# State-space stage of a two-block model: paired head products, a third weight buffer, exponents formed by ScalarE, convolutions in another PSUM pair, the gate applied ahead of the norm

## The chip, the cores and the metric

The kernel runs on one core of one Trainium2 chip. The metric is device time in microseconds (us) of one execution, as the median of several runs. The engines are TensorE (PE for its matmuls, PEld for its weight loads), VectorE (DVE), ScalarE (ACT), GpSimd (POOL) and the queue engine SyncE (SP), which issues every transfer here.

## The reference

The input is a sequence of 512 tokens of width 1024. A first block of two layers (windowed attention, two recurrent mixers, a gated feed-forward part) is followed by a second block of two layers. Each layer of the second block has three branches that are gated and added; the first is a state-space branch, and nearly all of the change lies there:

```python
def _ssd_branch(z, xbc, dt_raw, conv_w, conv_b, dt_bias, a_log, d_skip, norm_w):
    xbc = jax.nn.silu(_centred_dwconv(xbc, conv_w, conv_b))      # 5 taps
    xs, bm, cm = ...                                             # 32 heads of 64; 4 groups of state 128
    dt = softplus(dt_raw + dt_bias)                              # 2 directions x 32 heads
    y_fwd = _ssd_scan(xs * dt[fwd], dt[fwd] * a[0], bm, cm)      # chunks of 128 tokens
    y_bwd = flip(_ssd_scan(flip(...)))
    y = y_fwd + y_bwd + d_skip * xs
    return _rmsnorm(y * silu(z), norm_w)
# in _ssd_scan, within a chunk: y_diag = (C B^T * exp(cum_q - cum_s)) x, causal
# across chunks:                y_off  = exp(cum) * C state
# in second_block: merged = sigmoid(gate) * (y_ssd @ w_br_ssd) + two other branches
```

## The kernel before

Activations are kept with features on the partitions and the 512 tokens along the free dimension. A projection (`proj`, `gemm_fm`) makes one tile of 128 features: its weights are loaded as one `wraw` tile of 128x1024 by SP, `split` makes a high part `whi` (a cast on ACT, L396) and a low part `wlo` (a subtraction on DVE, L397), and PE runs 24 matmuls (three for each of 8 pieces of the contraction, L403 to L405) into a PSUM bank. There are three `wraw` buffers and two buffers each for `whi` and `wlo`. PSUM has three rings: `pg` of 2 banks (all projections), `pm` of 4 banks and `pb` of 2 banks.

The state-space stage (`ssd`) of a layer has these parts:

- `decays`: a small projection for the step sizes, the running sums of the decays, and their copies in DRAM (`d_fe`, `d_eo`) and token-major in SBUF (`tm`: `fet`, `dtt`, `dst`).
- `conv_x(g)` and `conv_bc(g)`: projections of 4 and 2 feature tiles for group g, each followed by `conv`: one ACT instruction out of PSUM (L1343), four DVE taps that read the same PSUM bank (L1348), and a Silu (L1349). All use the `pg` ring.
- `prelude(g)`: transposes (`pb` ring), the products C B^T masked both ways (`cbl`, `cbu`), and the recurrence over chunks (`xd`, L1473; the matmul L1475; `shd` and `shs`).
- `ftiles(g)`: four feature tiles of two heads each. A feature tile makes a `z` projection, and for each of its two heads (j = 0, 1) it loads two rows of running sums broadcast to 128 partitions (`rf`, `re`, 256 KB each, L1502 and L1503), forms the exponent tile `t1` chunk by chunk (POOL: row minus column for one direction, L1507; DVE: the other direction and the minimum of both, L1508), forms `t2` as the masked products with the step sizes (POOL L1509, DVE L1510), takes the exponential (ACT, L1511), multiplies (DVE, L1512), and runs four matmuls of 128x64 weights and 128 columns into the half `64 * j` of the partitions of one PSUM bank (L1515). After both heads come the skip term (L1518), the part across chunks (matmuls L1524, DVE L1527, POOL L1528), the gate with silu(z) (POOL L1531), the split of the result into `syp` (ACT L1533, DVE L1534) and its square (ACT L1540).
- `branch(g)`: the projection of the group's four tiles to the 8 tiles of `merged` (weights `ws`, DVE L1554 adds out of PSUM).
- At the end the norm's factor is made into a broadcast tile `rb`. L1576 (POOL) multiplies the eight gate tiles by it, and L1577 (DVE) multiplies `merged` by the result.

`weave` sets the order in which instructions are written: `ftiles(g)` together with `conv_x(g + 1)`, or for the last group with the eight gate projections; then `conv_bc(g + 1)`; then `prelude(g + 1)` together with `branch(g)`. A planner with a cost model then orders each engine's instructions, so that what is ready may run ahead of what was written earlier; on the chip each engine keeps that order. Attention in the first block has one line that the change touches, the product with the values at L1166.

Of the kernel before, what the change touches and what calls it, by code (L numbers as in the profile page):

```python
# [214 lines left out]
def bc(ap, axis, n):  # L215
# [21 lines left out]
    "scd": 1, "stm": 3, "svy": 2, "sbm": 1, "scm": 2, "sxf": 7, "sbt": 1, "scl": 1, "scu": 1, "sxt": 4, "sxd": 2, "shs": 6, "shd": 2,  # L237
    "seo": 1, "srf": 2, "sre": 2, "sy1": 1, "so1": 1, "szs": 3, "syp": 5, "sqa": 1, "ssq": 1,
# [42 lines left out]
class Core:  # L281
    def __init__(self, tc, es, wflat, wat):
        self.tc, self.nc = tc, tc.nc
        self.wflat, self.wat = wflat, wat
        self.sb = es.enter_context(tc.tile_pool(name="sb", bufs=1))
        self.cur, self.opened = None, []
        self.use("N")
        self.dr = es.enter_context(tc.tile_pool(name="dr", bufs=1, space=bass.MemoryType.DRAM))
        self.n = 0
        self.rr = 0  # L290

# [83 lines left out]
    def load(self, key, kt, stay=False, eng=None, bufs=4):  # L375

        raw = self.raw(key, "wraw", 3)
        shape = [P, self.wat[key][1]]
        if stay:
            hi, lo = (self.w(shape, F32R, name=t, b=bufs) for t in ("wkh", "wkl"))  # L380
        else:
            hi, lo = (self.keep(t, [P, W_SLOT], F32R, bufs=2)[:, : shape[1]] for t in ("whi", "wlo"))
        self.split(raw, hi, lo, eng)
        v = lambda a: a.rearrange("p (k c) -> p k c", k=kt)
        return v(hi), v(lo)
# [79 lines left out]
def block1(c: Core, io, consts, finish, kvs, stop=None):  # L465
# [619 lines left out]
    def mixer_a(l, raw, av, mixed, shared):  # L1085
# [64 lines left out]
        def values(t, w):  # L1150
            kts = [t - 1, t] if t else [t]
            for kv in range(2):
# [11 lines left out]
                for j in range(2):  # L1164
                    for i, u in enumerate(kts):
# [155 lines left out]
def block2(c: Core, io, C, h, out, kvs, stop=None):  # L1321
# [29 lines left out]
    def proj(l, key, h):  # L1351
        ps = c.pg()
        c.gemm_fm(c.load(key, KD), h, ps)
        return ps
# [10 lines left out]
    def decays(l, h, cdr, tm, d_fe, d_eo):  # L1365
# [45 lines left out]
        for k, src in enumerate((fe, dtT, ds_)):  # L1411
# [3 lines left out]
            V.tensor_copy(tm[k], pt)  # L1415
            yield

    def ssd(l, h, merged):
# [10 lines left out]
        def conv_x(g):  # L1429
            for i in range(4):  # L1430
                o = c.w(name="sxf")
                conv(proj(l, ("xbc", l, 4 * g + i), h), cw, cb, 4 * g + i, o)
# [9 lines left out]
        def prelude(g):  # L1442
# [25 lines left out]
            for n in range(3):  # L1468
                for d in range(2):
                    ch = (n, 3 - n)[d]  # L1470
                    r0 = 32 * d + 8 * g
                    xd = c.w(name="sxd")
# [14 lines left out]
        def ftiles(g):  # L1487
            s = grp[g]
            xf, xt, hs, cmf, cbl, cbu = s["xf"], s["xt"], s["hs"], s["scm"], s["cbl"], s["cbu"]
            for i in range(4):  # L1490
                f = 4 * g + i
                eo = c.w([P, 2, S], name="seo")
                for d in range(2):
                    for j in range(2):
                        nc.sync.dma_start(eo[64 * j : 64 * j + 64, d], d_eo[32 * d + 2 * f + j].partition_broadcast(64))
                zs = c.w(name="szs")
                A.activation(zs, proj(l, ("z", l, f), h), AF.Silu)
                py = c.pm()
                for j in range(2):
# [4 lines left out]
                    t1, t2 = c.w(name="st1"), c.w(name="st2")  # L1504
                    for ch in range(NT):
                        sl = slice(ch * P, (ch + 1) * P)
                        G.tensor_scalar(t1[:, sl], re[:, sl], -1.0, fet[:, ch, 32 + hh : 33 + hh], op0=ALU.mult, op1=ALU.add)  # L1507
                        V.scalar_tensor_tensor(t1[:, sl], rf[:, sl], fet[:, ch, hh : hh + 1], t1[:, sl], op0=ALU.subtract, op1=ALU.min)  # L1508
                        G.tensor_scalar(t2[:, sl], cbl[:, ch], dtt[:, ch, hh : hh + 1], 1.0, op0=ALU.mult, op1=ALU.mult)  # L1509
                        V.scalar_tensor_tensor(t2[:, sl], cbu[:, ch], dtt[:, ch, 32 + hh : 33 + hh], t2[:, sl], op0=ALU.mult, op1=ALU.add)  # L1510
                    A.activation(t1, t1, AF.Exp)  # L1511
                    V.tensor_tensor(t2, t1, t2, op=ALU.mult)  # L1512
                    for ch in range(NT):
                        sl = slice(ch * P, (ch + 1) * P)
                        T.matmul(py[64 * j : 64 * j + 64, sl], xt[ch][:, i * P + 64 * j : i * P + 64 * j + 64], t2[:, sl], start=True, stop=True)  # L1515
                    yield
                y1 = c.w(name="sy1")
                V.scalar_tensor_tensor(y1, xf[i], C(f"dsk{l}")[:, f : f + 1], py, op0=ALU.mult, op1=ALU.add)  # L1518
                for d in range(2):
# [7 lines left out]
                    V.tensor_tensor(o1, po.rearrange("p n t -> p (n t)"), eo[:, d, sl], op=ALU.mult)  # L1527
# [31 lines left out]
        with c.phase("ssd"):  # L1559
# [13 lines left out]
            rb = c.w(name="srb", b=1)  # L1573
            V.tensor_copy(rb, rbp)
            for m in range(KD):
                G.tensor_tensor(gates[m], gates[m], rb, op=ALU.mult)  # L1576
                V.tensor_tensor(merged[m], merged[m], gates[m], op=ALU.mult)  # L1577

# [528 lines left out]
```

## Time and profile before

| | |
|---|---|
| Time, median of 3 runs (lowest to highest) | 3928.01 us (3925.15 to 3929.15) |
| The profiled execution | 3929.44 us; its span from first to last instruction 3927.6 us |
| Busy over the span | PE 3667.1 us (93%), DVE 2471.0 us (63%), ACT 1655.0 us (42%), POOL 891.4 us (23%) |
| Mean granted clock of TensorE | 0.974 of full speed |
| State-space stage | about 1590 to 2085 us in the first layer of the second block, 2775 to 3285 us in the second |

A fp32 matmul of this kernel stands as two instructions in the trace, one of the `whi`/`wlo` projections as one. Busy time is the union of instructions, and matmuls overlap at their ends, so a busy PE is not one at its peak.

### The profile page before, as it was taken

What the parts mean: (1) busy time and instruction counts of PE and PEld (TensorE: products, weight loads), DVE (VectorE), ACT (ScalarE), POOL (GpSimd) and SP (SyncE); (2) the same over time, 40 slices, a digit from 0 to 9 for tenths busy, and PEclk for the clock granted to TensorE, in tenths of its full rate; (3) what the DMA queues carried; (4) which work ended last, traced back from release to release, by engine and by line L of the source; (5) the groups of instructions that cost most, each with busy time, mean ns of one, the idle gap of its engine ahead of it and who ended that gap; (6) DMA issues with size and microseconds to landing.
All of it is one profiled execution on the core that took longest, in us unless ns stands there. A gap on an engine that the chain in (4) does not pass through costs nothing. (4 is left out here: it accounts for less than half of the span.)

```text
span 3927.6 us, 51381 instructions
## 1 busy us (share of the span) xinstructions
PE 3667.1 (93%) x19000; PEld 3002.9 (76%) x19000; DVE 2471.0 (63%) x4543; ACT 1655.0 (42%) x2650; POOL 891.4 (23%) x1133
## 2 busy tenths in 40 slices
PE   6889999998889999899999999998989999999997
PEld 5776887787768888677777787877777777787877
DVE  7976645567665333778766674337677866765337
ACT  5432422245324223544444564333444444655333
POOL 1331000003210000245542111004245542111003
PEclk9989999999799999999999999999999999999999
DMA  6611445642113223443433332322443433332222
GB/s 192 188 54 46 142 158 191 207 141 68 33 49 110 97 97 102 121 135 118 135 108 99 97 105 81 102 81 97 149 128 129 129 113 98 104 100 81 102 81 86
DMA packets 167564, 437.64 MB, mean 111 GB/s; under 512 B 30096, under 2 KB 41744, under 8 KB 167312
## 3 DMA queue, kind: packets, MB, share of 16 engines
q1 hardware_dynamic: 167312, 434.34, 35.0%
q8 instruction: 150, 2.46, 0.3%
q14 instruction: 102, 0.84, 0.1%
HBM read 400.96 MB, written 12.32 MB: 105 GB/s over the span
## 5 line engine op out<-in xcount | busy, mean ns | idle before, releaser
L403 PE MATMUL pg<-h,whi 128*128 128x512 f32 x2624 | 1057.0, 403 | 58.1 <-ACT whi L396 27.1
L405 PE MATMUL pg<-h,wlo 128*128 128x512 f32 x2624 | 1039.9, 396 | 13.9 <-DVE wlo L397 13.8
L404 PE MATMUL pg<-h,whi 128*128 128x512 f32 x2624 | 1037.5, 395 | 3.4 <-POOL h L397 3.4
L396 ACT CAST whi<-wraw 128x1024 fp32r<-128x1024 f32 (+1 forms) x532 | 552.1, 1039 | 1144.7 <-PE pg L404 927.0
L397 DVE TENSOR_TENSOR wlo<-wraw,whi 128x1024 fp32r<-128x1024 f32 (+1 forms) x532 | 701.1, 1319 | 435.9 <-ACT whi L396 423.9
L403 PEld LDWEIGHTS pg<-h,whi 128*128 128x128 f32 x2624 | 497.8, 190 | 176.1 <-ACT whi L396 41.3
L405 PEld LDWEIGHTS pg<-h,wlo 128*128 128x128 f32 x2624 | 497.5, 190 | 131.1 <-DVE wlo L397 25.8
L404 PEld LDWEIGHTS pg<-h,whi 128*128 128x128 f32 x2624 | 498.3, 190 | 112.0 <-POOL h L397 6.5
L397 POOL TENSOR_TENSOR gp<-mraw,gp 128x256 fp32r<-128x256 f32 x32 | 26.1, 833 | 866.5 <-ACT gp L396 866.5
L403 PE MATMUL pg<-whi,h 128*128 128x256 f32 (+1 forms) x640 | 189.6, 298 | 11.2 <-ACT whi L396 8.6
L404 PE MATMUL pg<-wlo,h 128*128 128x256 f32 (+1 forms) x640 | 187.6, 294 | 9.9 <-DVE wlo L397 9.8
L405 PE MATMUL pg<-whi,h 128*128 128x256 f32 (+1 forms) x640 | 185.4, 290 | 0.0
L1509 POOL TENSOR_SCALAR st<-scl,stm 128x128 f32<-128x128 f32 x256 | 121.9, 491 | 203.8 <-DVE scl L1463 127.7
L1507 POOL TENSOR_SCALAR st<-sre,stm 128x128 f32<-128x128 f32 x256 | 117.1, 469 | 199.3 <-DMA sre<-dram 124.6
L405 PE MATMUL pg<-gp,wlo 128*128 128x512 f32 (+1 forms) x432 | 160.0, 370 | 0.9 <-DVE wlo L397 0.9
L403 PE MATMUL pg<-gp,whi 128*128 128x512 f32 (+1 forms) x432 | 159.7, 370 | 0.0
L404 PE MATMUL pg<-gp,whi 128*128 128x512 f32 (+1 forms) x432 | 159.6, 369 | 0.0
L1348 DVE SCALAR_TENSOR_TENSOR svy<-pg,c,svy 128x510 f32<-128x510 f32 x192 | 142.5, 742 | 18.3 <-ACT svy L1343 16.9
L403 PE MATMUL pg<-yp,whi 128*128 128x512 f32 (+1 forms) x384 | 144.8, 379 | 4.8 <-ACT yp L396 2.9
L405 PE MATMUL pg<-yp,wlo 128*128 128x512 f32 (+1 forms) x384 | 144.4, 378 | 4.0 <-DVE wlo L397 4.0
L404 PE MATMUL pg<-yp,whi 128*128 128x512 f32 (+1 forms) x384 | 144.5, 377 | 3.7 <-DVE yp L397 3.7
L403 PEld LDWEIGHTS pg<-whi,h 128*128 128x128 f32 x640 | 125.9, 198 | 18.2 <-ACT whi L396 10.8
(558 smaller groups left out, 6733.5 us busy)
## 6 DMA issues: line engine op xcount, KB each, us to landing
wraw<-in_wflat_dram SPq DMA_DIRECT2D x596, 512.0 KB
srf<-dram SPq DMA_DIRECT2D x64, 256.0 KB
sre<-dram SPq DMA_DIRECT2D x64, 256.0 KB
seo<-dram SPq DMA_DIRECT2D x128, 128.0 KB
araw<-in_wflat_dram SPq DMA_DIRECT2D x16, 512.0 KB
rsw<-rr SPq DMA_DIRECT2D x128, 64.0 KB
wraw<-in_wflat_dram SPq DMA_DIRECT2D x16, 384.0 KB
mraw<-in_mem_dram SPq DMA_DIRECT2D x40, 128.0 KB
```

Of the source, the lines that this page charges most:

```text
L396: self.nc.scalar.copy(hi, src)
L397: (eng or self.nc.vector).tensor_tensor(lo, src, hi.bitcast(F32), op=ALU.subtract)
L403: mm(out, ah, bh, start=start, stop=False)
L404: mm(out, ah, bl, start=False, stop=False)
L405: mm(out, al, bh, start=False, stop=stop)
L1348: V.scalar_tensor_tensor(y[:, d], ps[:, s], cw[:, tap, m : m + 1], y[:, d], op0=ALU.mult, op1=ALU.add)
L1507: G.tensor_scalar(t1[:, sl], re[:, sl], -1.0, fet[:, ch, 32 + hh : 33 + hh], op0=ALU.mult, op1=ALU.add)
L1509: G.tensor_scalar(t2[:, sl], cbl[:, ch], dtt[:, ch, hh : hh + 1], 1.0, op0=ALU.mult, op1=ALU.mult)
```

## The change

- L1166 (first block): the loops over the key blocks and over the two halves `j` change places.
- `ftiles`: the four matmuls of each head move behind both heads' exponent work, and the two heads alternate, so that neighbours write different halves of the partitions.
- `load`: while the stage runs, every third weight load takes a third pair of buffers (`xhi`, `xlo`).
- The exponents: eight ACT instructions (Identity with a bias per partition, four with scale -1) for each head, in place on `re` and `rf`, then one DVE minimum of 128x512, and the exponential in place. The POOL line L1507 and the DVE line L1508 go. The columns of `fet` for the first direction are negated once in `decays`.
- `conv_x` projects into the `pb` ring; `conv_bc` stays in `pg`.
- `merged` is multiplied by the gate on DVE first, then by `rb` on POOL; `rb` takes the buffer of `sy1`.
- `eo` holds and loads the three chunks in use instead of four. Buffers: `sre` 3 for 2, `st2` 4 for 2 (it also serves as `xd`), `syp` 4 for 5; `st1`, `sxd` and `srb` go.

```diff
-    "scd": 1, "stm": 3, ... "sxt": 4, "sxd": 2, "shs": 6, "shd": 2,
-    "seo": 1, "srf": 2, "sre": 2, "sy1": 1, "so1": 1, "szs": 3, "syp": 5, "sqa": 1, "ssq": 1,
+    "scd": 1, "stm": 3, ... "sxt": 4, "shs": 6, "shd": 2,
+    "seo": 1, "srf": 2, "sre": 3, "st2": 4, "sy1": 1, "so1": 1, "szs": 3, "syp": 4, "sqa": 1, "ssq": 1,
...
+        elif self.spare and next(self.spare_turn) == 2:
+            hi, lo = (self.w(shape, F32R, name=t, b=1, pool=self.spare) for t in ("xhi", "xlo"))
...
-                for j in range(2):
-                    for i, u in enumerate(kts):
+                for i, u in enumerate(kts):
+                    for j in range(2):
                         T.matmul(ps[64 * j : 64 * j + 64]..., av[u][...], pT[i][:, j]..., start=i == 0, stop=i == len(kts) - 1)
...
-    def proj(l, key, h):
-        ps = c.pg()
+    def proj(l, key, h, bank="pg"):
+        ps = c.psum(bank, (P, S))
...
-            V.tensor_copy(tm[k], pt)
+            if k == 0:
+                V.tensor_scalar(tm[k][:, :, 0:32], pt[:, :, 0:32], -1.0, None, op0=ALU.mult)
+                V.tensor_copy(tm[k][:, :, 32:64], pt[:, :, 32:64])
+            else:
+                V.tensor_copy(tm[k], pt)
...
-                conv(proj(l, ("xbc", l, 4 * g + i), h), cw, cb, 4 * g + i, o)
+                conv(proj(l, ("xbc", l, 4 * g + i), h, "pb"), cw, cb, 4 * g + i, o)
...
-                    xd = c.w(name="sxd")
+                    xd = c.w(name="st2")
...
-                eo = c.w([P, 2, S], name="seo")
+                eo = c.w([P, 2, 3 * P], name="seo")
...
-                    t1, t2 = c.w(name="st1"), c.w(name="st2")
+                    t2 = c.w(name="st2")
                     for ch in range(NT):
                         sl = slice(ch * P, (ch + 1) * P)
-                        G.tensor_scalar(t1[:, sl], re[:, sl], -1.0, fet[:, ch, 32 + hh : 33 + hh], op0=ALU.mult, op1=ALU.add)
-                        V.scalar_tensor_tensor(t1[:, sl], rf[:, sl], fet[:, ch, hh : hh + 1], t1[:, sl], op0=ALU.subtract, op1=ALU.min)
+                        A.activation(re[:, sl], re[:, sl], AF.Identity, scale=-1.0, bias=fet[:, ch, 32 + hh : 33 + hh])
+                        A.activation(rf[:, sl], rf[:, sl], AF.Identity, bias=fet[:, ch, hh : hh + 1])
                         G.tensor_scalar(t2[:, sl], cbl[:, ch], dtt[:, ch, hh : hh + 1], 1.0, op0=ALU.mult, op1=ALU.mult)
                         V.scalar_tensor_tensor(t2[:, sl], cbu[:, ch], dtt[:, ch, 32 + hh : 33 + hh], t2[:, sl], op0=ALU.mult, op1=ALU.add)
-                    A.activation(t1, t1, AF.Exp)
-                    V.tensor_tensor(t2, t1, t2, op=ALU.mult)
-                    for ch in range(NT):
-                        sl = slice(ch * P, (ch + 1) * P)
-                        T.matmul(py[64 * j : 64 * j + 64, sl], xt[ch][:, i * P + 64 * j : i * P + 64 * j + 64], t2[:, sl], start=True, stop=True)
+                    V.tensor_tensor(re, rf, re, op=ALU.min)
+                    A.activation(re, re, AF.Exp)
+                    V.tensor_tensor(t2, re, t2, op=ALU.mult)
+                    att.append(t2)
                     yield
+                for ch in range(NT):
+                    sl = slice(ch * P, (ch + 1) * P)
+                    for j in range(2):
+                        T.matmul(py[64 * j : 64 * j + 64, sl], xt[ch][:, i * P + 64 * j : i * P + 64 * j + 64], att[j][:, sl], start=True, stop=True)
...
-        with c.phase("ssd"):
+        with c.phase("ssd") as pool:
+            c.spare, c.spare_turn = pool, cycle(range(3))
...
-            rb = c.w(name="srb", b=1)
+            rb = c.w(name="sy1")
             V.tensor_copy(rb, rbp)
             for m in range(KD):
-                G.tensor_tensor(gates[m], gates[m], rb, op=ALU.mult)
                 V.tensor_tensor(merged[m], merged[m], gates[m], op=ALU.mult)
+                G.tensor_tensor(merged[m], merged[m], rb, op=ALU.mult)
+            c.spare = None
```

## Rows read from the trace of the kernel before

**Rows 1.** Page, engine totals: busy us (share of the span) and instructions.
```profile
PE 3667.1 (93%) x19000; PEld 3002.9 (76%) x19000; DVE 2471.0 (63%) x4543; ACT 1655.0 (42%) x2650; POOL 891.4 (23%) x1133
```

**Rows 2.** Windows of the two state-space stages: busy us (instructions), clock, DMA.
```profile
1590.00:2085.00 495.00, 452.22 (x2122) 353.83 (x2122) 376.92 (x630) 236.47 (x291) 235.88 (x343) 0.98 0.38 118
2775.00:3285.00 510.00, 474.78 (x2255) 373.43 (x2254) 385.30 (x639) 235.87 (x293) 239.67 (x344) 0.99 0.38 121
```

**Rows 3.** Waits of PE in the first stage: us, times, longest.
```profile
PE pg L403 <- ACT whi L396: 11.5, 7, 2.6
PE pg L403 <- DVE svy L1348: 10.9, 7, 4.0
...
PE pm L1515 <- DVE st L1512: 1.1, 3, 0.4
```

**Rows 4.** Windows: three tiles of group 1, then group 3 whole (columns as above).
```profile
1778.90:1796.20 17.30, 14.73 (x76) 11.89 (x77) 16.01 (x30) 8.63 (x12) 12.99 (x21) 1.00 0.45 157
1796.20:1814.10 17.90, 16.39 (x76) 13.01 (x76) 15.57 (x29) 8.70 (x12) 13.39 (x21) 0.90 0.47 145
1814.10:1831.50 17.40, 17.36 (x85) 14.37 (x86) 10.83 (x18) 10.04 (x13) 8.25 (x9) 1.00 0.41 126
...
1968.60:2060.00 91.40, 88.59 (x424) 70.25 (x425) 58.27 (x91) 45.68 (x50) 44.95 (x62) 0.98 0.37 116
```

**Rows 5.** Timeline of ACT at the end of the first of them: start, length.
```profile
1793.90 0.72 ACT L1533 ACTIVATE syp<-szs,c 128x512 fp32r<-128x512 f32 x1 [5.60 <-POOL szs L1531]
1794.53 0.61 ACT L1540 ACTIVATE ssq<-szs 128x512 f32<-128x512 f32 x1
1795.05 1.03 ACT L396 CAST whi<-wraw 128x1024 fp32r<-128x1024 f32 x1
```

**Rows 6.** Timeline of PE just after: the next projection.
```profile
1796.21 0.47 PE L403 MATMUL pg<-h,whi 128*128 128x512 f32 x1 [2.56 <-ACT whi L396]
```

**Rows 7.** Groups by line, DVE, 1778.9 to 1814.1: busy, mean ns, idle before.
```profile
L1508 DVE SCALAR_TENSOR_TENSOR st<-srf,stm,st 128x128 f32<-128x128 f32 x16 | 5.9, 428 | 0.0
...
L1512 DVE TENSOR_TENSOR st<-st,st 128x512 f32<-128x512 f32 x4 | 2.8, 711 | 0.1
```

**Rows 8.** The same for POOL.
```profile
L1507 POOL TENSOR_SCALAR st<-sre,stm 128x128 f32<-128x128 f32 x16 | 6.6, 425 | 0.8 <-DVE st L1512 0.8
```

**Rows 9.** Groups by line and shape, ACT, whole span.
```profile
L1511 ACT ACT_TABLE_LOAD x41 | 52.6, 1283 | 30.5 <-DVE st L1508 29.9
...
L1343 ACT ACTIVATE svy<-pg,c 128x512 f32<-128x512 f32 x48 | 36.8, 768 | 1.4 <-PE pg L405 1.4
...
L574 ACT ACTIVATE hq<-pb 128x128 f32<-128x128 f32 x16 | 4.5, 278 | 18.3 <-PE pb L1030 14.3 <-PE pb L1027 3.9
...
L1139 ACT ACTIVATE asc<-asc,As 128x128 f32<-128x128 f32 x8 | 3.1, 388 | 0.0
```

**Rows 10.** Timeline of PE, one head's products, then a first-block product in halves.
```profile
1886.80 1.09 PE L1515 MATMUL pm<-st,sxt 128*64 128x128 f32 x8
...
339.50 0.66 PE L824 MATMUL pm<-c,ckg 128*64 128x128 f32 x8
```

**Rows 11.** Timeline of PE, the product L1166 with the values.
```profile
317.69 1.09 PE L1166 MATMUL pg<-apT,av 128*64 128x256 f32 x8 [0.78 <-DVE apT L1161]
```

**Rows 12.** Timeline of DVE, POOL and PE at the end of the first stage.
```profile
2073.10 12.72 POOL L1576 TENSOR_TENSOR sxf<-sxf,srb 128x512 f32<-128x512 f32 x8 [10.03 <-DVE srb L1574]
2074.43 5.10 DVE L1577 TENSOR_TENSOR mg<-mg,sxf 128x512 f32<-128x512 f32 x3 [1.41 <-POOL sxf L1576]
...
2079.46 0.67 DVE L1554 TENSOR_TENSOR mg<-mg,pg 128x512 f32<-128x512 f32 x1
...
2080.28 0.50 PE L403 MATMUL pg<-syp,whi 128*128 128x512 f32 x1 [4.73 <-DVE mg L1554]
```

**Rows 13.** Waits of the SP queue in the first stage.
```profile
SPq L1503 <- POOL st L1507: 122.2, 28, 18.6
```

More of the change, by code (lines that the diff above doesn't have):

```diff
@@ L2 @@
 from contextlib import ExitStack
-from itertools import chain
+from itertools import chain, cycle
 import numpy as np
@@ L235 @@
     "ar": 4, "av": 4, "akT": 4, "asc": 4, "apT": 2, "aqT": 2, "As8": 16,
-    "scd": 1, "stm": 3, "svy": 2, "sbm": 1, "scm": 2, "sxf": 7, "sbt": 1, "scl": 1, "scu": 1, "sxt": 4, "sxd": 2, "shs": 6, "shd": 2,
-    "seo": 1, "srf": 2, "sre": 2, "sy1": 1, "so1": 1, "szs": 3, "syp": 5, "sqa": 1, "ssq": 1,
+    "scd": 1, "stm": 3, "svy": 2, "sbm": 1, "scm": 2, "sxf": 7, "sbt": 1, "scl": 1, "scu": 1, "sxt": 4, "shs": 6, "shd": 2,
+    "seo": 1, "srf": 2, "sre": 3, "st2": 4, "sy1": 1, "so1": 1, "szs": 3, "syp": 4, "sqa": 1, "ssq": 1,
     "dv": 8, "hs": 8, "ls": 4, "lq": 1, "dp": 4, "dtw": 1, "don": 1, "dsg": 2, "dy": 1, "Ds8": 26,
@@ L290, in __init__ @@
         self.rr = 0
+        self.spare, self.spare_turn = None, None
     def phase(self, name, banks=None):
@@ L1491, in ftiles @@
                 f = 4 * g + i
-                eo = c.w([P, 2, S], name="seo")
+                eo = c.w([P, 2, 3 * P], name="seo")
                 for d in range(2):
+                    ch = slice((1 - d) * P, (4 - d) * P)
                     for j in range(2):
-                        nc.sync.dma_start(eo[64 * j : 64 * j + 64, d], d_eo[32 * d + 2 * f + j].partition_broadcast(64))
+                        nc.sync.dma_start(eo[64 * j : 64 * j + 64, d], d_eo[32 * d + 2 * f + j, ch].partition_broadcast(64))
                 zs = c.w(name="szs")
                 A.activation(zs, proj(l, ("z", l, f), h), AF.Silu)
-                py = c.pm()
+                py, att = c.pm(), []
                 for j in range(2):
@@ L1526, in ftiles @@
                     sl = slice(c0 * P, c0 * P + 3 * P)
-                    V.tensor_tensor(o1, po.rearrange("p n t -> p (n t)"), eo[:, d, sl], op=ALU.mult)
+                    V.tensor_tensor(o1, po.rearrange("p n t -> p (n t)"), eo[:, d], op=ALU.mult)
                     G.tensor_tensor(y1[:, sl], y1[:, sl], o1, op=ALU.add)
```

## Prediction

> **What bounds the kernel now.** I read the page first, then windows by stage, then PE's waits in the stage that the change touches, then single feature tiles. The page shows PE busy 93% of the span and no other engine over 63% [rows 1]. So whatever frees another engine is worth only what PE stands still for it, and the question is how long PE stands still in the two state-space stages. The windows answer: 495 - 452 = 43 us in the first and 510 - 475 = 35 us in the second [rows 2]. These 78 us, and PE work that is taken out, are all there is to win, with some clock on top.
>
> The waits name the places: PE waited for the cast `whi` and for the convolution's taps `svy`, 11.5 and 10.9 us in the first stage, and only 1.1 us for the heads' products themselves [rows 3]. The tiles show the pattern. A feature tile of group 1 takes 17.3 to 17.9 us, in which DVE is busy 15.6 to 16.0 us, POOL 13.0 to 13.4, ACT 8.6 to 8.7, PE 14.7 in the first [rows 4]. There DVE sets the pace, not PE: the reader is to see an engine at 63% of the whole span that is at 90% of this stretch. How it reaches PE is in the timeline: ACT stands 5.60 us before the split of `syp`, because that waits for POOL, and the cast of the next weights is queued behind it; PE then stands 2.56 us [rows 5, 6]. In the tile that follows such a stop the granted clock is 0.90 instead of 1.00 and much the same work keeps PE busy 16.39 instead of 14.73 us: 1.7 us more [rows 4]. The last tile of a group, and group 3 with its gate projections, are another case: PE is busy 17.36 of 17.40 us, and 88.6 of 91.4 [rows 4]. There only PE work counts.
>
> **Paired head products.** Eight instructions of one head take 1.09 us; eight instructions of the same shape that go to both halves of the partitions take 0.66 us in the first block [rows 10]. Two heads cost 2.18 us now; by the lower row 2 x 0.66 = 1.32, at best 1.09. That saves 0.86 to 1.09 us a tile; I take 1.0. Cost: the first head's products now wait for the second's. PE runs in its order, so the projection queued behind them waits too, and behind that the taps, and behind the products the skip term L1518. Today that wait is 1.1 us in a stage [rows 3]; I add nothing and keep it as a rival. L1166: the eight instructions of the unchanged order already stand in 1.09 us with twice the columns [rows 11], so they already run two abreast; I take 0, between 0 and 3 us.
>
> **Exponents.** For each of two heads a tile loses four POOL instructions of 425 ns and four DVE instructions of 428 ns, and gains eight ACT instructions of 128x128 and one DVE minimum, priced as L1512 at 711 ns [rows 7, 8].
> - DVE: 15.8 - 8 x 0.428 + 2 x 0.711 = 13.8 us a tile.
> - POOL: 13.2 - 8 x 0.425 = 9.8 us.
> - PE: 14.7 - 1.0 = 13.7 us.
> - ACT: the nearest rows are 278 ns (no bias per partition, from PSUM) and 388 ns (bias per partition, in place in SBUF) [rows 9]. The second is the nearer in its operands, but ACT starts an instruction some 0.09 us before the one ahead has ended (0.61 us from 1794.53, next at 1795.05 [rows 5]), so 0.30 is possible; I take 0.34. ACT: 8.7 + 16 x 0.34 = 14.1 us, between 13.1 and 14.9. Identity brings no table load: L1343 is an Identity, and no load stands at its line [rows 9].
>
> So four engines end up between 9.8 and 14.1 us, three of them nearly level, and ACT becomes the fullest. Today a tile takes 17.6 us where the fullest engine has 15.8; I keep that remainder of 1.8, since in-order waits do not go away with three level engines: 14.1 + 1.8 = 15.9 us. That is 1.7 us less for a tile that DVE paces. There are 18 of those (three in each of groups 0 to 2, two layers): 31 us. The six last tiles of these groups are PE's: 6 x 1.0 = 6 us.
>
> Against the move to ACT speaks a rule. First the rows: they price the arithmetic at 428 ns on DVE and up to 388 ns on ACT for the same 128x128 [rows 7, 9], so the trace makes ACT no dearer per piece. The Trainium skill, ScalarE: Activation LUTs, section Rules for kernel authors, says to use VectorE, not ScalarE, for add, multiply and minimum. By that rule the change goes the wrong way; by the rows the piece costs about the same and moves from an engine with 1.5 us free in the tile to one with 8.9 us free.
>
> **Third weight buffer.** It lets a cast run one projection ahead, so the cast need not stand behind the `syp` split. In the 18 tiles that gain is part of the step from 17.6 to 15.9. In group 3 it takes most of 91.4 - 88.6 = 2.8 us [rows 4]: 2 us in each layer, and the pairing 4 x 1.0: 2 x 6 = 12 us. The casts cost the same as before.
>
> **Convolutions in the other PSUM pair.** A tap pass no longer holds a `pg` bank. Within tiles this is counted already; outside them the longest wait is 4.0 us, at the stage's start [rows 3]. `conv_bc` stays in `pg`. I take 2 us a layer, 4 together; 0 to 8.
>
> **Gate ahead of the norm.** At the end of the first stage DVE runs L1577 behind POOL's L1576, three in 5.10 us, and the addition L1554 that frees a `pg` bank is queued behind them: PE stands 4.73 us [rows 12]. Afterwards DVE's multiplication needs no POOL result, and POOL's eight multiplications (12.7 us together) come last, where only a much later addition reads them. I take 5 us for both layers; 0 to 9. Nothing is late next but the first projections of the next branch, which read no gate.
>
> **Buffers and transfers.** `re` is now held until the product is formed, against a third buffer; `rf` until the minimum. SP today waits 122 us for POOL to release `re` [rows 13], and weight loads queue behind it, yet PE's waits show no weight transfer [rows 3]; 15 us a tile and two to three buffers cover it. The smaller `eo`, four `syp` for five, `xd` in `st2`'s ring and the negated `fet` columns (one more DVE instruction a layer) I cost at nothing; if `xd` must wait for products, it is about a microsecond a group.
>
> **Sum.** 31 + 6 + 12 + 4 + 5 = 58 us, against the profiled execution: 3929.4 - 58 = 3871. The median of the runs is 1.4 us lower: 3870.
>
> **Bounds.** Best: the 18 tiles run at PE's 13.7 us, 18 x 3.9 = 70, with 6 + 12 + 8 + 9 + 3 for the rest: 108 us, 3820. Worst without a new wait: ACT at 388 ns, 14.9 + 1.8 = 16.7 us, 18 x 0.9 = 16, with 6 + 12: 34 us, 3894.
>
> **Rivals.**
> - ACT becomes the pace. 41 loads of the exponential's table stand for 64 heads [rows 9]; if each head needs its own, one more of 1.28 us falls in a tile, ACT has 14.9 + 1.3 = 16.2, and with the remainder 18.0 us. The 18 tiles then lose 0.4 each; with 27 us kept elsewhere: 3929 - 20 = 3909. For it: three functions share that engine in one order. Against: ACT stood 8.9 us of 17.6. Chance 0.20. The rule of the Trainium skill above would lead here.
> - PE becomes the pace everywhere: 3820 to 3840. For it: DVE, ACT and PE within half a microsecond and one more buffer. Against: the remainder above. Chance 0.12.
> - The joint wait (the other side). If the second head's product is late on PE in each of the 24 tiles of groups 0 to 2, each stop takes its length and about 1.7 us of clock, as after the stop of 2.56 [rows 4, 6]. It decides from 58 / 24 = 2.4 us a tile; a stop of 2.0 gives 24 x 3.7 = 89, so 3929 - 58 + 89 = 3960. For it: the chain ACT, DVE, ACT, DVE is longer than before and PE's order is fixed. Against: 1.1 us of such waits now, and four `st2` buffers. Chance 0.13.
> - The products do not pair at this place. That takes the pairing's 6 + 8 = 14 us off, 3884, within my own range.
>
> **Chances.** My forecast (3840 to 3895) 0.53, ACT as pace 0.20, PE as pace 0.12, the joint wait 0.13, nothing visible 0.02. A measurement tells 0.2%, some 8 us, from no change. Faster by more 0.82 (0.53 + 0.12 + 0.17), the same 0.05, slower 0.13. The range 3828 to 3912 leaves out the joint wait and the best end.
>
> **What would show it.** Right: windows of a tile at 15 to 16.5 us with ACT near 14, DVE near 14, POOL near 10; sixteen L1515 instructions in 1.1 to 1.4 us; PE's waits for `whi` in the stage down from 11.5 to a few; no PE stop beside the last L1554. Wrong: tiles still at 17 us with ACT busy over 16; PE waiting for the products at L1515 by more than 2 us a tile; or weight transfers among PE's and ACT's waits.

## The result and the profile after

The changed kernel takes 3862.57 us (median of 4 runs, 3858.31 to 3867.21) against 3926.58 us of the kernel before on the same chip (4 runs, 3923.80 to 3929.15): ratio 0.9837, 95% interval 0.9826 to 0.9849, some 64 us faster. The forecast was 3870. Its profiled execution has a span of 3860.2 us against 3927.6. Line numbers moved: the casts are L400 and L401, the projections L407 to L409, the exponents L1517 (`re`) and L1518 (`rf`), the two summed products L1519 (POOL) and L1520 (DVE), the minimum L1521, the exponential L1522, the paired products L1529, the skip term `y1` L1531, `o1` and its addition L1540 and L1541, `yz` L1544, the split of `syp` L1546 and L1547.

The page's totals: PE 40 us less, POOL 123 less, ACT 144 more.

```profile
PE 3627.2 (94%) x19000; PEld 2984.8 (77%) x19000; DVE 2427.1 (63%) x4353; ACT 1798.9 (47%) x3159; POOL 768.1 (20%) x877
```

Windows of the two state-space stages, each from its first decay step to the first instruction of the next branch (length, then busy PE, PEld, DVE, ACT, POOL with instructions, clock, DMA share, GB/s):

```profile
1586.20:2049.70 463.50, 440.03 (x2177) 352.46 (x2178) 356.54 (x538) 307.89 (x547) 166.46 (x211) 0.97 0.41 124
2740.20:3214.10 473.90, 450.23 (x2208) 361.31 (x2207) 357.70 (x539) 306.04 (x543) 169.90 (x212) 0.96 0.40 122
```

The same two stretches of the kernel before:

```profile
1595.40:2099.30 503.90, 464.73 (x2177) 364.51 (x2178) 380.08 (x635) 237.83 (x294) 236.70 (x343) 0.98 0.38 118
2783.30:3283.60 500.30, 465.08 (x2201) 366.21 (x2201) 382.16 (x636) 232.80 (x289) 238.91 (x343) 0.99 0.38 120
```

Length less PE's busy time is how long PE stands: 39.2 and 35.2 us before, 23.5 and 23.7 after. The rest of the gain is PE's own work, 24.7 and 14.9 us less. The paired products make 14.1 us of it in each stage (e7 below). The other 10.6 us of the first stage lie in the `h` projections, 1157 instructions that keep PE busy for 457 us instead of 469; no run here explains them.

PE's waits in the first stage, answering to [rows 3]:

```profile
PE pg L407 <- DVE svy L1352: 7.1, 3, 5.4
PE pb L407 <- ACT xhi L400: 5.7, 1, 5.7
PE pb L429 <- ACT sxt L1458: 4.6, 2, 4.1
PE pb L429 <- ACT sxf L1353: 3.8, 1, 3.8
PE pm L1529 <- DVE st L1523: 2.7, 1, 2.7
...
PE pg L407 <- DVE mg L1567: 0.7, 2, 0.4
```

The waits for `whi` are gone (the one for `xhi`, 5.7 us, stands at the stage's start); new are the transposes L429 between two groups, which wait for ACT: for the Silu of the tile that they read (L1353) and for the copies that empty their bank (L1458). Before the longest of these waits in the first stage ACT itself stands for the convolution's taps, and between the Silu and the copies it runs the split, the square, two convolution instructions and two casts (timeline of ACT):

```profile
1904.24 1.28 ACT L1353 ACT_TABLE_LOAD   x1 [2.02 <-DVE svy L1352]
...
1910.42 1.06 ACT L1458 COPY sxt<-pb 128x512 f32<-128x512 f32 x2
```

In the second stage these two waits are 17.0 us.

Windows of the tiles of group 1, `y1` to `y1`, and of the passage to the next group, answering to [rows 4]:

```profile
1745.70:1764.60 18.90, 18.90 (x107) 15.82 (x107) 14.97 (x25) 16.30 (x35) 13.69 (x20) 1.00 0.45 145
1764.60:1777.60 13.00, 13.00 (x76) 10.73 (x75) 12.47 (x22) 11.07 (x21) 4.58 (x4) 1.00 0.42 122
1777.60:1791.20 13.60, 13.60 (x78) 11.23 (x77) 11.56 (x14) 12.00 (x24) 5.26 (x4) 1.00 0.66 194
1791.20:1849.30 58.10, 52.27 (x233) 40.43 (x232) 45.46 (x70) 28.83 (x52) 17.23 (x25) 0.94 0.34 104
...
1799.00:1804.40 5.40, 0.06 (x1) 0.02 (x1) 4.76 (x6) 5.37 (x9) 1.31 (x1) 0.77 0.52 156
1804.40:1810.00 5.60, 5.43 (x16) 4.13 (x16) 1.78 (x2) 3.80 (x6) 0.00 (x0) 0.61 0.49 169
```

The same three intervals of the kernel before, cut from `y1` to `y1` too:

```profile
1770.09:1786.93 16.84, 15.99 (x89) 13.15 (x89) 15.23 (x29) 9.82 (x14) 13.81 (x23) 1.00 0.40 114
1786.93:1804.61 17.68, 15.12 (x68) 11.76 (x66) 15.49 (x29) 8.87 (x12) 12.65 (x18) 0.90 0.47 145
1804.61:1820.92 16.31, 14.77 (x77) 11.89 (x78) 12.19 (x19) 8.92 (x12) 9.29 (x12) 1.00 0.48 160
```

PE is now busy all of every tile of groups 1 and 2, in both stages, at full clock; in group 0 it still stands 2.8 us in the first stage and 2.1 in the second, and the clock of its tiles is 0.93 to 1.00. Over all 18 intervals PE's busy time is the same, 274.9 us before and 275.7 after; its standing went from 32.9 us to 4.9. What it stands, 5.8 us here, lies in the passage between groups. There PE stood 5.36 us for the taps, and in the 5.6 us that follow, with PE busy again, the granted clock is 0.61, mostly the lower of its two levels.

Where the 67.4 us between the two spans lie, from the starts of the 16 `y1` instructions of each stage (us, first and second stage):

| stretch | before | after | gained | terms of the forecast |
|---|---|---|---|---|
| stage's start to the first `y1` | 63.2, 61.9 | 57.9, 64.7 | 2.6 | convolutions 4 |
| nine intervals inside groups 0 to 2 | 152.9, 154.9 | 142.4, 138.2 | 27.3 | 18 tiles, 31 |
| three passages between groups | 178.0, 177.9 | 169.0, 175.4 | 11.5 | last tiles 6 |
| group 3, and the last `y1` to the next stage or the end | 793.8, 749.5 | 784.8, 741.7 | 16.8 | group 3 and gate, 17 |

The sum is 58.2. The other 9.2 us lie ahead of the first stage, which starts at 1595.4 us before and at 1586.2 after. Among the profiles of all kernels here it starts between 1577.2 and 1595.4, and two kernels with the same first block (below, the unpaired one and the one with the minimum in four parts) have it at 1594.4 and 1577.2: most of that part is not the change. L1166 lies in it, with 4 us less of PE's work (e1).

### The profile page after: what moved, and what is told of

It is laid out like the page before. It is cut to its first block, busy times and chain, and to the rows that moved or that the text cites. A ratio compares the mean times of both kernels' runs of the same rounds, so it can differ in the third digit from the quotient of the medians.

```text
span 3860.2 us, 51317 instructions
## 1 busy us (share of the span) xinstructions
PE 3627.2 (94%) x19000; PEld 2984.8 (77%) x19000; DVE 2427.1 (63%) x4353; ACT 1798.9 (47%) x3159; POOL 768.1 (20%) x877
## 5 line engine op out<-in xcount | busy, mean ns | idle before, releaser
L400 ACT CAST whi<-wraw 128x1024 fp32r<-128x1024 f32 (+1 forms) x490 | 508.6, 1039 | 1044.4 <-PE pg L408 846.8
L401 DVE TENSOR_TENSOR wlo<-wraw,whi 128x1024 fp32r<-128x1024 f32 (+1 forms) x490 | 644.2, 1316 | 415.2 <-ACT whi L400 397.0
L407 PE MATMUL pg<-h,whi 128*128 128x512 f32 (+1 forms) x2192 | 877.8, 401 | 14.6 <-ACT h L400 10.9
L409 PE MATMUL pg<-h,wlo 128*128 128x512 f32 (+1 forms) x2192 | 862.8, 394 | 6.5 <-DVE wlo L401 6.4
L408 PE MATMUL pg<-h,whi 128*128 128x512 f32 (+1 forms) x2192 | 863.2, 394 | 3.9 <-POOL h L401 3.9
L407 PEld LDWEIGHTS pg<-h,whi 128*128 128x128 f32 (+1 forms) x2192 | 413.1, 189 | 106.7 <-ACT h L400 13.6
L409 PEld LDWEIGHTS pg<-h,wlo 128*128 128x128 f32 (+1 forms) x2192 | 413.1, 188 | 99.9 <-DVE wlo L401 13.7
L408 PEld LDWEIGHTS pg<-h,whi 128*128 128x128 f32 (+1 forms) x2192 | 413.5, 189 | 94.4 <-POOL h L401 7.0
L407 PE MATMUL pg<-whi,h 128*128 128x256 f32 (+1 forms) x640 | 189.6, 298 | 12.6 <-ACT whi L400 7.5
L401 POOL TENSOR_TENSOR gp<-mraw,gp 128x256 fp32r<-128x256 f32 x32 | 25.5, 816 | 863.1 <-ACT gp L400 863.1
L409 PE MATMUL pg<-whi,h 128*128 128x256 f32 (+1 forms) x640 | 185.5, 290 | 0.0
L409 PE MATMUL pg<-gp,wlo 128*128 128x512 f32 (+1 forms) x432 | 159.9, 370 | 0.9 <-DVE wlo L401 0.9
L407 PE MATMUL pg<-gp,whi 128*128 128x512 f32 (+1 forms) x432 | 159.7, 370 | 0.0
L407 PE MATMUL pg<-yp,whi 128*128 128x512 f32 (+1 forms) x384 | 145.3, 380 | 4.7 <-ACT yp L400 2.9
L409 PE MATMUL pg<-yp,wlo 128*128 128x512 f32 (+1 forms) x384 | 144.8, 379 | 4.1 <-DVE wlo L401 4.1
L1519 POOL TENSOR_SCALAR st<-scl,stm 128x128 f32<-128x128 f32 x256 | 124.9, 507 | 89.2 <-PE pm L1529 89.2
L407 PEld LDWEIGHTS pg<-whi,h 128*128 128x128 f32 x640 | 125.9, 198 | 20.2 <-ACT whi L400 10.1
L408 PEld LDWEIGHTS pg<-wlo,h 128*128 128x128 f32 x640 | 126.3, 198 | 15.1 <-DVE wlo L401 12.8
L530 DVE CUSTOM_DVE_ANT_0 wraw<-wraw,cond 128x1024 f32<-128x1024 f32 x80 | 99.8, 1254 | 55.2 <-DMA wraw<-in_wflat_dram 55.1
```

The lines of the kernel that those rows point to most:

```text
L400: self.nc.scalar.copy(hi, src)
L401: (eng or self.nc.vector).tensor_tensor(lo, src, hi.bitcast(F32), op=ALU.subtract)
L407: mm(out, ah, bh, start=start, stop=False)
L408: mm(out, ah, bl, start=False, stop=False)
L409: mm(out, al, bh, start=False, stop=stop)
L530: V.tensor_tensor_reduce(r, r, cond, 1.0, 0.0, ALU.mult, ALU.add, mod[:, j : j + 1])
```

## The experiments

Each was timed in five rounds beside the kernel before on the same chip; 0.001 of a ratio is 3.9 us. The last column is PE's standing time in the two stages, by windows as above.

| kernel | us | ratio, 95% interval | PE stands |
|---|---|---|---|
| changed kernel | 3862.57 | 0.9837 (0.9826 to 0.9849) | 23.5, 23.7 |
| e1 before + L1166's loops | 3921.70 | 0.9995 (0.9986 to 1.0004) | 39.0, 35.2 |
| e2 before + third weight buffer | 3921.26 | 0.9993 (0.9984 to 1.0002) | 35.8, 34.3 |
| e3 after, two weight buffers | 3875.70 | 0.9881 (0.9868 to 0.9895) | 31.1, 26.0 |
| e4 after, old exponents | 3923.50 | 0.9994 (0.9985 to 1.0003) | 41.7, 42.9 |
| e5 after, two buffers and old exponents | 3932.17 | 1.0022 (1.0013 to 1.0031) | 51.3, 41.0 |
| e6 before + exponents on ACT | 3905.16 | 0.9950 (0.9938 to 0.9963) | 31.4, 24.8 |
| e7 after, products unpaired | 3881.33 | 0.9887 (0.9872 to 0.9902) | 17.1, 16.3 |
| e8 after, `re` by POOL, rest as after | 3922.11 | 0.9997 (0.9987 to 1.0007) | 44.8, 50.3 |
| e9 after, minimum in four by DVE | 3873.88 | 0.9867 (0.9853 to 0.9881) | 27.8, 29.6 |
| e10 after, convolutions in `pg` | 3858.68 | 0.9836 (0.9823 to 0.9850) | 24.4, 24.0 |
| e11 after, old gate order | 3860.43 | 0.9837 (0.9824 to 0.9851) | 27.3, 24.8 |
| e12 as e9, no POOL in the heads | 3859.98 | 0.9827 (0.9814 to 0.9841) | 23.2, 20.0 |

**e1.**
```diff
-                for j in range(2):
-                    for i, u in enumerate(kts):
+                for i, u in enumerate(kts):
+                    for j in range(2):
```


> The kernel before with the two loops at L1166 exchanged and nothing else. The prediction's term: 0, between 0 and 3 us, as the products ran two abreast already. The rival from the trace after, in which the stage begins 9.2 us earlier: the line alone gives 9 us, about 3917; if those 9 us come from elsewhere, the time stays within 2 us of before.

The whole run can't tell it: 2 us, with an interval of 3.5 to either side. PE's work at the line does shrink, from 23.6 us of busy time for its 112 instructions to 18.4 here and 19.3 in the changed kernel. The instructions of [rows 11] ran two abreast already, but others did not: in the last three groups of each layer, eight instructions took 0.65 + 1.08 us and now take 0.65 + 0.65 (timeline of PE, before and then e1):

```profile
341.13 0.65 PE L1166 MATMUL pg<-apT,av 128*64 128x256 f32 x2
342.66 1.08 PE L1166 MATMUL pg<-apT,av 128*64 128x256 f32 x6
```

```profile
336.07 0.65 PE L1166 MATMUL pg<-apT,av 128*64 128x256 f32 x4
337.61 0.65 PE L1166 MATMUL pg<-apT,av 128*64 128x256 f32 x4
```

**e2.** The third weight buffer alone (room made by the smaller `eo`, four `syp`, `xd` and `rb` in other rings).
```diff
+        elif self.spare and next(self.spare_turn) == 2:
+            hi, lo = (self.w(shape, F32R, name=t, b=1, pool=self.spare) for t in ("xhi", "xlo"))
```


> The kernel before with the third pair of weight buffers in the state-space stage alone (room for it from four syp buffers, a smaller eo, rb in sy1's buffer and xd in a ring of three st2 buffers). My theory, in which VectorE paces the tiles: only the stops for the cast go, 10 to 20 us, 3907 to 3917. The rival, in which the cast behind the syp split paces them: 35 us or more, 3890 or below.

Nothing gained that can be told: PE's wait for `whi` falls from 11.5 us to 2.8, it stands for the taps `svy` instead (14.4 us, 11 times; 10.9 before) and 5.7 us for the new `xhi`. A wait was moved, not removed.

**e3.** The same buffer taken from the changed kernel.
```diff
-            c.spare, c.spare_turn = pool, cycle(range(3))
```


> The kernel after without the third pair of weight buffers. My theory: the stops for the cast come back in part, 10 to 20 us slower than after, 3873 to 3883. The rival, in which the buffer carries the change: 35 us or more, 3898 or above.

Here the buffer is worth 17 us by the ratios (13 by the medians). PE's waits without it, in the first stage:

```profile
PE pb L409 <- DVE wlo L401: 11.5, 7, 2.8
PE pb L429 <- ACT sxt L1458: 9.1, 3, 4.2
```

**e4.** The exponents of before, written in place on `re`.
```diff
-                        A.activation(re[:, sl], re[:, sl], AF.Identity, scale=-1.0, bias=fet[:, ch, 32 + hh : 33 + hh])
-                        A.activation(rf[:, sl], rf[:, sl], AF.Identity, bias=fet[:, ch, hh : hh + 1])
+                        G.tensor_scalar(re[:, sl], re[:, sl], -1.0, fet[:, ch, 32 + hh : 33 + hh], op0=ALU.mult, op1=ALU.add)
+                        V.scalar_tensor_tensor(re[:, sl], rf[:, sl], fet[:, ch, hh : hh + 1], re[:, sl], op0=ALU.subtract, op1=ALU.min)
...
-                    V.tensor_tensor(re, rf, re, op=ALU.min)
```


> The kernel after with the exponents formed as before (four POOL and four VectorE instructions of 128x128 for each head, now in place on re, no minimum and no negated fet), all else as after. My theory, VectorE as pace: a tile goes back to about 17 us, 18 tiles by 1.0 to 1.7 us, 18 to 30 us slower than after, 3880 to 3893. The rival, in which the move to ScalarE gives nothing or costs: 3858 to 3866.

All of the gain is gone: 62 us, twice the most that the theory allowed. The pairing is still there (PE busy 452.5 and 459.0 us in the stages, 12 and 6 less than before), but PE stands longer and its clock is 0.95 in both stages.

**e5.** e3 with the exponents of before, in a buffer `t1` of their own as there: what is left of the change is pairing, `pb`, gate and L1166.

> The kernel after without the third weight buffers and with the exponents exactly as before, in t1 tiles of their own; what stays are the paired products, the convolutions in the other PSUM pair, the gate order and the buffer counts. Beside e3, which differs in the exponents alone. My theory (VectorE paced the tiles, so pairing and the PSUM pair show little while it does): 3905 to 3922. The rival, in which e4 lost only because re was held longer in place: 3878 to 3892.

Slower than before by 9 us, and 55 slower than e3, so the exponents' worth doesn't hang on whether they are formed in place. PE's waits in the first stage, in which the low halves of the weights now come late:

```profile
PE pb L409 <- DVE wlo L401: 20.6, 7, 4.8
PE pg L409 <- DVE wlo L401: 9.8, 7, 2.3
```

**e6.** The kernel before with the exponents of after (and three `sre`).

> The kernel before with the exponents formed by ScalarE (and three sre buffers) alone; heads unpaired, convolutions in pg, two weight buffers. My theory: most of the gain is here, 25 to 45 us, 3880 to 3900. The rival, in which the cast of the weights now waits behind a fuller ScalarE and the gain needs the other edits: 3912 or above.

20 us. The waits for `whi` are gone as in the full change, but the taps take their place: `svy` 18.2 us, 12 times.

**e7.**
```diff
-                    att.append(t2)
+                    for ch in range(NT):
+                        sl = slice(ch * P, (ch + 1) * P)
+                        T.matmul(py[64 * j : 64 * j + 64, sl], xt[ch][:, i * P + 64 * j : i * P + 64 * j + 64], t2[:, sl], start=True, stop=True)
```


> The kernel after with each head's four products behind that head's exponents, as before. TensorE fills the tiles of the kernel after to 100 per cent, so the pairing's 1.0 us a tile should show in all 32 tiles: 20 to 32 us slower than after, 3882 to 3895. The rival, that two heads' products run side by side anyway or another engine paces: 3860 to 3870.

The pairing is worth 20 us. PE's products of the heads take 33.6 us a stage before and 19.5 after, so PE was relieved of 28 us; some of it came back as standing time, 33.4 us in both stages unpaired and 47.2 paired. This is the changed kernel's group, sixteen instructions in the time of eight of [rows 10] (timeline of PE: start, length):

```profile
2010.97 1.09 PE L1529 MATMUL pm<-st,sxt 128*64 128x128 f32 x16
```

**e8 and e9.** The two halves of the exponents' move apart. e8 gives `re` back to POOL and leaves DVE its one minimum; e9 leaves `re` to ACT and gives DVE its four instructions back, in place of four on ACT and the minimum.
```diff
-                        A.activation(re[:, sl], re[:, sl], AF.Identity, scale=-1.0, bias=fet[:, ch, 32 + hh : 33 + hh])
+                        G.tensor_scalar(re[:, sl], re[:, sl], -1.0, fet[:, ch, 32 + hh : 33 + hh], op0=ALU.mult, op1=ALU.add)
```
```diff
-                        A.activation(rf[:, sl], rf[:, sl], AF.Identity, bias=fet[:, ch, hh : hh + 1])
+                        V.scalar_tensor_tensor(re[:, sl], rf[:, sl], fet[:, ch, hh : hh + 1], re[:, sl], op0=ALU.subtract, op1=ALU.min)
...
-                    V.tensor_tensor(re, rf, re, op=ALU.min)
```


> The kernel after with the re row formed by POOL (as before, in place) and the rf row by ScalarE, minimum on VectorE as after: ScalarE gets 3.1 us a tile less, POOL 3.4 us more. Theory: the stops between groups (transposes behind ScalarE) shrink, 8 to 20 us faster than after, 3843 to 3855. The rival: POOL beside VectorE slows VectorE's two-input work again and the tiles lose what the change gave: 3865 or above.

> The kernel after with the re row formed by ScalarE as after, and the rf row and the minimum by four VectorE instructions of 128x128 as before (fet not negated). The counterpart of e8: VectorE's load goes back to that of before (about 2 us a tile more than after), POOL stays free of exponents, ScalarE has 3.1 us a tile less. If VectorE's load is what the change relieved: 3895 to 3920. If POOL's place in the chain is: within 10 us of after, 3850 to 3870.

e8 gains nothing, though it was expected to be 8 to 20 us faster than the changed kernel, and though DVE is exactly as free as after (356.1 us busy in the first stage, 356.5 after). e9 keeps some 52 of the 64 us although DVE has all its instructions back (367 us busy in each stage; 380 and 382 before). With e4 and the changed kernel these are the four ways to share the exponents, in an otherwise equal kernel (ratio; then the sum of the 18 intervals inside groups, 307.8 us before):

| | DVE forms the second row and the minimum | ACT forms the second row, DVE one minimum |
|---|---|---|
| POOL forms `re` | e4: 0.9994; 313.9 us | e8: 0.9997; 305.4 us |
| ACT forms `re` | e9: 0.9867; 287.4 us | changed kernel: 0.9837; 280.6 us |

Taking `re` from POOL is worth 50 to 63 us by the ratios, relieving DVE nothing to 12. It is POOL's part that counts. How it reaches the path in e8, in a tile whose `y1` starts at 1774.04 (timeline of POOL: start, length, what ended the idle time before):

```profile
1774.75 2.81 POOL L1519 TENSOR_SCALAR st<-scl,stm 128x128 f32<-128x128 f32 x8
1777.56 0.37 POOL L1517 TENSOR_SCALAR sre<-sre,stm 128x128 f32<-128x128 f32 x1
1777.90 1.01 POOL L1541 TENSOR_TENSOR sy<-sy,so 128x384 f32<-128x384 f32 x1
1778.91 1.07 POOL L1517 TENSOR_SCALAR sre<-sre,stm 128x128 f32<-128x128 f32 x3
1779.95 1.00 POOL L1541 TENSOR_TENSOR sy<-sy,so 128x384 f32<-128x384 f32 x1
1781.03 2.15 POOL L1544 TENSOR_TENSOR szs<-sy,szs 128x512 f32<-128x512 f32 x1
```

DVE in between:

```profile
1775.35 0.54 DVE L1540 TENSOR_TENSOR so<-pm,seo 128x384 f32<-128x384 f32 x1
...
1778.94 0.56 DVE L1540 TENSOR_TENSOR so<-pm,seo 128x384 f32<-128x384 f32 x1 [2.39 <-POOL sy L1541]
```

The first `o1` is ready at 1775.89. POOL adds it 2.0 us later, because it is still at the next heads' products and exponents; DVE stands 2.39 us for the one buffer of `o1`; and `yz`, on which the split and the squares wait, starts 7.0 us after `y1`. The same in the changed kernel, `y1` at 1764.60:

```profile
1766.57 1.01 POOL L1541 TENSOR_TENSOR sy<-sy,so 128x384 f32<-128x384 f32 x1 [2.00 <-DVE so L1540]
1768.24 1.01 POOL L1541 TENSOR_TENSOR sy<-sy,so 128x384 f32<-128x384 f32 x1 [0.67 <-DVE so L1540]
1769.33 1.29 POOL L1544 TENSOR_TENSOR szs<-sy,szs 128x512 f32<-128x512 f32 x1
```

There POOL waits for DVE, and `yz` starts 4.7 us after `y1`. At the mean of groups 0 to 2 this distance is 6.4 us in e8 and 5.9 in e4, against 5.1 in the changed kernel and 4.9 in e9. In the kernel before, however, it is 5.0: the tile of [rows 5], with `y1` at 1786.93, had POOL waiting for DVE as well (timeline of POOL):

```profile
1788.28 1.02 POOL L1528 TENSOR_TENSOR sy<-sy,so 128x384 f32<-128x384 f32 x1 [0.69 <-DVE so L1527]
1790.65 1.01 POOL L1528 TENSOR_TENSOR sy<-sy,so 128x384 f32<-128x384 f32 x1 [1.35 <-DVE so L1527]
1791.73 2.13 POOL L1531 TENSOR_TENSOR szs<-sy,szs 128x512 f32<-128x512 f32 x1
```

So this queue explains e8 and e4, and not the long tiles of the kernel before. Over a stage: ACT's and DVE's waits behind POOL in e8,

```profile
ACT syp L1546 <- POOL szs L1544: 34.0, 14, 6.7
DVE so L1540 <- POOL sy L1541: 27.6, 16, 4.1
```

against the changed kernel's

```profile
ACT syp L1546 <- POOL szs L1544: 24.5, 10, 4.6
DVE so L1540 <- POOL sy L1541: 11.0, 15, 1.5
```

and the kernel before's

```profile
ACT syp L1533 <- POOL szs L1531: 81.2, 16, 6.0
DVE so L1527 <- POOL sy L1528: 5.4, 10, 0.9
```

Both waits over both stages make 177 us before (gain 0), 194 in e2 (gain 3), 185 in e4 (2), 157 in e5 (a loss of 9), 145 in e8 (1), 94 in e6 (20), 92 in e9 (52), 84 in e7 (44), 75 in e3 (47) and 66 in the changed kernel (64). They fall roughly as the time does, but they don't measure a late `yz`: it comes no earlier after `y1` in the changed kernel than before, and ACT's wait for it is shorter there while ACT has 70 us more work in the stage. What holds POOL up besides its work is the first instruction of each head, which in e8 waits for the transfer of `re` (36.5 us, 14 times), often with the additions of the tile before queued behind it.

**e10 and e11.** The convolutions back in `pg`; the gate's old order.
```diff
-                conv(proj(l, ("xbc", l, 4 * g + i), h, "pb"), cw, cb, 4 * g + i, o)
+                conv(proj(l, ("xbc", l, 4 * g + i), h), cw, cb, 4 * g + i, o)
```
```diff
+                G.tensor_tensor(gates[m], gates[m], rb, op=ALU.mult)
                 V.tensor_tensor(merged[m], merged[m], gates[m], op=ALU.mult)
-                G.tensor_tensor(merged[m], merged[m], rb, op=ALU.mult)
```


> The kernel after with the convolutions' projections in the pg ring again. The prediction's term was 4 us, 0 to 8. From e6, where TensorE waited 18.2 us in a stage for the taps once the exponents were on ScalarE: 25 to 40 us slower than after, 3888 to 3903. The rival, the prediction's term: 3863 to 3870.

> The kernel after with the gate tiles multiplied by the norm factor on POOL first, as before. The prediction's term: 5 us, 0 to 9, so 3863 to 3872. The rival: nothing, because the queue at the end of the stage is another one in the kernel after: 3860 to 3864.

Neither can be told from the changed kernel, to about 7 us, so the 25 to 40 us expected of e10 did not come. In e10 PE does wait for the taps again (17.8 and 15.7 us in the two stages), but hardly for the transposes (1.6 and 2.8); its standing time stays the same. In e11's profile the stop of [rows 12] is back, to the hundredth (timeline of PE):

```profile
2040.19 0.77 PE L407 MATMUL pg<-syp,whi 128*128 128x512 f32 x1 [4.73 <-DVE mg L1567]
```

and the stretch from the last `y1` to the next stage is 732.4 us for 727.1; so the edit does its 5 us at that place in the first stage, and a whole run can't show it.

**e12.** e9, and the first of the two summed products of a head goes from POOL to ACT. POOL then has no part in a head before its additions; ACT carries its heavier load and DVE its heavier one.
```diff
-                        G.tensor_scalar(t2[:, sl], cbl[:, ch], dtt[:, ch, hh : hh + 1], 1.0, op0=ALU.mult, op1=ALU.mult)
+                        A.mul(t2[:, sl], cbl[:, ch], dtt[:, ch, hh : hh + 1])
```


> Kernel: the one of the run before (subtracted exponents by ScalarE, the other side and the minimum by VectorE), and the first of the two summed products of each head (t2) goes from GpSimd to ScalarE: GpSimd has then no part in a head before its gate. ScalarE takes 8 instructions of 388 ns a head instead of 4 (the load of the changed kernel), VectorE 8 instead of 4 (the load of the kernel before). Theory that GpSimd's place in the chain of each head is what the exponents' move relieved: as fast as the changed kernel or faster, 3850 to 3865 us. Rival, that VectorE's and ScalarE's loads together pace the tiles when both carry the heavier of their two loads: 3875 to 3890. Rival, that any of these three allocations is as good as the next: 3860 to 3875.

As fast as the changed kernel (the intervals overlap; 0.9827 against 0.9837), and 16 us faster than e9 by the ratios. The two waits behind POOL are down to 53 us over both stages. Tiles of its group 1:

```profile
1750.40:1765.90 15.50, 15.50 (x91) 13.02 (x92) 13.68 (x28) 11.73 (x27) 5.54 (x4) 1.00 0.41 117
1765.90:1781.90 16.00, 16.00 (x89) 13.21 (x88) 13.61 (x30) 12.80 (x27) 5.00 (x4) 1.00 0.51 163
```

PE is again busy throughout. So DVE could keep every instruction of before; they take 362 and 366 us of its time in the stages, against 380 and 382 before.

## Why the prediction was right, and where its reason was wrong

**The total held; that its parts agree is in part luck.** 58 us were forecast, 58.2 lie in the two stages and behind them, and 64 by the medians. The 18 intervals inside groups became 1.5 us shorter each (1.7 forecast), and tiles mean 15.6 us (15.9 forecast). But an interval is no fixed piece of work: in e7, 20 us slower than the changed kernel, the 18 take 270.0 us, 10.6 less than there, and the six passages 369.2, 24.8 more. And the last row of the table agrees only as a sum: group 3's own three intervals gave 2.2 of its 16.8 us, where the sum had most of 12 for the group, and the stretch behind the last `y1` gave 14.6, where the gate's 5 were expected.

**The step that failed is "There DVE sets the pace, not PE".** The rows showed DVE busy for 90% of a tile and, in the same group of rows, ACT standing 5.60 us behind POOL [rows 4, 5]; the sum was built on the first and used the second only to tell how the stop reaches PE. e4, e8, e9 and e12 show in its place that POOL's part in forming the exponents holds the tiles: with DVE as light as after and POOL at `re` nothing is gained, with all of DVE's instructions back and POOL out of the heads all of it is. DVE's lighter load is worth at most the 12 us between e9 and the changed kernel, and e12 has that back without it. POOL was no idle engine there: 13.0 us busy of the 17.3 of a tile [rows 4], though 23% of the span. The forecast came out because the same edit frees both engines: that is luck. The four ways were tried in the changed kernel only; in the kernel before, e6 shows that the whole move shortens the 18 intervals as far (279.9 us), and no run took its halves apart there.

**The remainder of 1.8 us failed too.** It was kept "since in-order waits do not go away with three level engines". Inside the tiles PE's did: it is busy 45.5 of 45.5 us in group 1's three, and 275.7 of 280.6 in all 18. That is what the rival with PE as the pace foresaw for the tiles; it missed on the whole because PE now stands between the groups, at the transposes, and because a tile holds more of PE's work than the 13.7 us that were reckoned: the three hold 15.2 us each at the mean, as they did before (15.3, by the same cut). What pairing took out of PE's work in a tile was filled with other work, and left the passages shorter.

**Engine loads.** ACT gained 70.1 us in the first stage, 4.4 a tile for 16 instructions, against 5.4 priced at 0.34 each. They last 391 ns each and start 0.30 us apart. POOL lost 4.4 us a tile (3.4 forecast), DVE 1.5 (2.0): the minimum took 813 ns and not 711. DVE's free time in a tile, which the prediction sets at 1.5 us, was 17.6 - 15.8 = 1.8. The exponential's table is loaded 41 times as before, so what the rival with ACT as the pace needed did not come:

```profile
L1517 ACT ACTIVATE sre<-sre,stm 128x128 f32<-128x128 f32 x256 | 95.0, 391 | 42.0 <-DMA sre<-dram 41.1 <-DVE st L1520 0.8
...
L1522 ACT ACT_TABLE_LOAD x41 | 52.6, 1283 | 10.5 <-DVE sre L1521 9.9
```

The Trainium skill's rule in ScalarE: Activation LUTs, Rules for kernel authors (VectorE, not ScalarE, for add, multiply and minimum), would have kept this work off ACT. Here the arrangements with eight such instructions a head on ACT (the changed kernel, e12) are the fastest; those with four are 12 us (e9) and 63 us (e8) slower. The rule speaks of one instruction's price; what decided here was which engine's queue it stands in.

**Pairing.** On PE 0.88 us a tile (1.0 forecast), 28 in all; 20 of it reach the end. The joint wait did not come: PE waits 2.7 and 2.5 us for the products in the two stages, 1.1 and 2.5 before.

**Third buffer.** 4 us in group 3 were forecast beside a part of the tiles; it is worth 17 with the other edits and nothing alone (e2).

**Convolutions, gate, L1166.** 4, 5 and 0 forecast. No whole run shows any of them; the gate's 5 us show at their place. For L1166 the prediction read "already run two abreast" from one row [rows 11], which did not hold for the line: PE's work there fell by 4 to 5 us (e1). How much of that reaches the end no run tells.

**The edits don't add.** Exponents alone 20 us; everything else without them 2 (e4), without the buffer too 9 slower (e5). With the exponents in place buffer and pairing add 17 and 20: 20 + 17 + 20 = 57 of 64. With the old exponents PE's saved work turns into standing time: in e4 PE is busy 18 us less than before in the two stages and stands 10 us more.

**Left open.** How POOL's part made the tiles of the kernel before long isn't shown: `yz` came no later there. In the first stage POOL stood 33.1 us there, 14 times, for the product L1512 to release `t1`; whether a further `t1` would have helped was not tried. Whether POOL could keep `re` if its transfer came earlier (a further buffer of `re`) was not tried: e8 doesn't separate POOL's work from its wait for the transfer. Why e5 stands so long for the low halves of the weights was not followed. The transposes between the groups, 8.4 and 17.0 us, are what the changed kernel still has to give in this stage.

## What to carry to other kernels

An engine that is 90% busy in a stretch is a suspect, not the culprit: look at which engine the waiting instructions name, even if its share of the whole span is small (POOL: 23% of the span, 75% of the tile), and move one half of an edit at a time to tell them apart. Work on an in-order engine that serves two ends of a chain, the start of the next item and the finish of the last, can delay the finish when the start has to wait, as in e8. Price edits together: a buffer or a saving on the bounding engine that is worth nothing alone can be worth 17 to 20 us once what hid it is gone.

## What the runs showed of the hardware

A DVE instruction with two operands in SBUF became longer when a POOL instruction ran beside it. The product of two 128x512 operands took 0.67 to 0.69 us wherever none did: 19 of 32 in the first stage before, 26 of 32 in e12, where POOL has almost left the heads. Those that overlapped one took 0.68 to 1.55 us, 0.94 at the mean of 13 before and 0.75 of 6 in e12. The three longest before end 0.54 to 0.55 us after the POOL instruction in which they began; one of them, and that POOL instruction:

```profile
2017.62 1.39 DVE L1512 TENSOR_TENSOR st<-st,st 128x512 f32<-128x512 f32 x1
```

```profile
2017.41 1.05 POOL L1528 TENSOR_TENSOR sy<-sy,so 128x384 f32<-128x384 f32 x1 [0.96 <-DVE so L1527]
```

The mean of all 32 falls with it, from 789 ns before to 694 in e12. It does not follow POOL's load alone, though: it is 755 ns after and 736 in e8, where POOL is busier (226 us of the stage against 166). The Trainium skill, SBUF — State Buffer, section Who interferes with whom, says that a DVE instruction with two SBUF inputs contends with a GpSimd instruction that reads SBUF; these durations agree. It is not what e8 lost by: DVE's busy time there is that of the changed kernel.
